# Five edits to a streaming encoder layer: silu applied in the query stage, work reordered in the first and third chunk, another bank for the latents' transposes, a later norm

## The chip, the cores and the metric

The kernel runs on one core of one Trainium2 chip. The core has a matrix engine (TensorE, PE in the profile; PEld is its weight load), a vector engine (VectorE, DVE), an activation engine (ScalarE, ACT), a general engine (GpSimd, POOL) and a sync engine (SyncE, SP) which issues most of the DMA transfers. Each has its own queue of instructions; the engines meet at semaphores. TensorE writes into PSUM, which here is divided into eight banks: four named `mm`, two named `tp` and two named `g`. The metric is the device time of one execution in microseconds (us); lower is better.

## The reference

One layer of a streaming encoder, for 1024 new frames of one stream (positions from 0) and 64 frames of a running stream with 512 cached frames. The model width is 1024; the two streams lie side by side as 1088 tokens.

```
mod = silu(c) @ w_ada + b_ada              # six vectors per stream: shift, scale, gate, twice
h = rms_norm(x, g_norm1) * (1 + scale1) + shift1
proj = h @ w_in                            # c_q 384, c_kv 256, k_rope 64, gq 256, gk 256, gv 512, g_lr 16, g_r 512
latent = rms_norm(c_kv);  q = rms_norm(c_q) @ w_uq;  k, v = latent @ w_ukv     # norms per head, rotary part
a_out = chunk-causal softmax attention(q, k, v)                # 4 heads, the cached frames ahead of the new ones
b_out = rms_norm(gated linear recurrence(gq, gk, gv, gate(g_lr))) * silu(g_r)
x = x + gate1 * (concat(a_out, b_out) @ w_out)
h2 = rms_norm(x, g_norm2) * (1 + scale2) + shift2
x = x + gate2 * (square(relu(h2 @ w_up)) @ w_down)
```

It returns x for both streams, the new latents and rotary keys, and the final states of the recurrence. Everything is float32.

## The kernel before

Almost every matmul is made three times: an operand is split into a rounded high part and the rest (`split`, lines 101 to 103: a copy on ACT, a subtraction on DVE), and `mm3` (lines 92 to 96) multiplies high by high, high by low and low by high into one PSUM bank. In the last stages `w_up` and `w_down` are multiplied by a scheme with seven products of half-size blocks.

**What sets the order.** The stages are written as Python generators that yield `(PE time, wait, condition)`; `interleave` (line 47) runs them by a clock of its own, in nanoseconds, and so fixes the order in which instructions are written down. A condition is a set of names that must be in `done`. Behind this, a scheduler lays out each engine's queue: an instruction written earlier has precedence, but one whose operands and buffers it takes to be ready may go ahead. So the load of line 619, which is written behind the whole first stage, is issued at 33.83 us. An instruction inside `pin` (`keep_in_program_order`) keeps its place among the pinned ones of its engine.

**First stage** (to about 90 us). The tokens come in three chunks of 384, 384 and 320 columns (`CHUNKS`). `start` loads the first chunk of x in two halves of four blocks of 128 rows each (`load_x`, line 301), the half-matrices of `w_ada` for the scale, and the first weights of groups A0 and A1 (`load_first`). `scale_rows` and `scale_end` (lines 466 and 472) make the scale in two halves: matmuls, a copy on ACT (line 474), a transpose on PE (line 478) and three small DVE operations that leave the gain G. Then `gained_x` (line 379) multiplies x by G into `hh` (ACT, line 383) and `hl` (DVE, line 384); `split_first` (line 324) splits weights (lines 328 and 329); `squares` (line 332) makes the squares of x on ACT and `adds` (line 338) sums them over the eight blocks on DVE (line 342); `scales` (line 345) turns the sums into the factor of the norm. `shifts` (line 491) makes the shift vector: `mod_vec` (line 158) loads rows of `w_ada` (line 165), three ahead, and multiplies them one after another (line 177); it also issues the load of the third chunk of x. `qk` (line 528) makes the first matmuls of all, for gq and gk.

**Recurrence, keys and queries** (about 90 to 350 us). `gate_cols` (line 676) makes the 512 columns of g_r and stores them in DRAM as `r_d`, unchanged. `latents` (line 686) normalises c_kv of one tile of 128 tokens after another, transposes it (line 710) into a PSUM bank, copies it out with a gain (line 713) and stores it. `past_keys` and `new_keys` make keys and values, with transposes into `tp` banks (lines 1001 and 1008). `query_main` (line 1321) makes c_q, 384 columns at a time. Small buffers of this stage lie in the pool `qp` (line 1355).

**Attention and output** (about 350 to 690 us). `attend` (line 1068) makes scores, their exponentials on ACT (line 1090), transposes of these (line 1116) and the product with the values. `out_early` (line 1273) and `main` (line 1411) load the mixed heads and `r_d`, apply silu to the latter and multiply (`gate`, line 1269), split the result and multiply it by `w_out`, in four parts of 272 tokens in the order `WORDER = (0, 2, 1, 3)`. While a part is made, squares of the new x are summed into `acc` (line 1465). `norm2` (line 1469) waits until a part is done and a time more, sums `acc` over the partitions on PE (line 1479) and spreads the factor of the norm (line 1490).

**Feed-forward** (about 690 us to the end). The seven products of `w_up` and of `w_down`; the diff does not touch them.

Of the kernel before, what the change touches and what calls it, by code (L numbers as in the profile page):

```python
# [19 lines left out]
P = 128  # L20
# [52 lines left out]
def layer(ctx: ExitStack, tc: tile.TileContext, I, O):  # L73
# [9 lines left out]
    def mm_bank():  # L83
        return psA.tile([P, 512], F32, name="mm")

    def tp_bank():
        return psT.tile([P, 512], F32, name="tp")
# [147 lines left out]
    def has(*keys):  # L235
        return lambda: all(k in done or k in groups for k in keys)
# [59 lines left out]
    with ExitStack() as sctx:  # L296
# [4 lines left out]
        def load_x(c, ks=(0, 4)):  # L301
            c0, cn = CHUNKS[c]
            for k in ks:
                SP.dma_start(hf[:, k:k + 4, c0:c0 + cn],
                             I["x_T"][k * P:(k + 4) * P, c0:c0 + cn].rearrange("(k p) n -> p k n", p=P))
# [18 lines left out]
        def split_first(hf, j, us=None):  # L324
            for u in us or (2 * hf, 2 * hf + 1):
                wh, wl = groups[GROUPS[j][0]]
                hi, lo, raw = wh[:, 2 * u:2 * u + 2], wl[:, 2 * u:2 * u + 2], first.pop((j, u))
                pin(ACT.copy(hi, raw))  # L328
                pin(DVE.tensor_tensor(out=lo, in0=raw, in1=f32(hi), op=ALU.subtract))
                done.add(f"split {j} {u}")  # L330

        def squares(c, sq, ks):

            c0, cn = CHUNKS[c]
            for k in ks:
                pin(ACT.activation(sq[:, k:k + 4, :cn], hf[:, k:k + 4, c0:c0 + cn], AF.Square))
# [42 lines left out]
        def gained_x(k, c, pin=lambda mm: mm):  # L379

            for s, a, b in spans(c):
                x, g = hf[:, k, a:b], G12[:, 0, k, s:s + 1]
                pin(ACT.activation(h["h"][:, k, a:b], x, AF.Copy, scale=g))
                mm = DVE.scalar_tensor_tensor(out=h["l"][:, k, a:b], in0=x, scalar=g, in1=f32(h["h"][:, k, a:b]),
                                              op0=ALU.mult, op1=ALU.subtract)
                if c == 0:
                    pin(mm)

        def start():
            load_mod(0)  # L390
            load_x(0, (0,))
            load_first(0)
            load_mod(1)
            load_x(0, (4,))
            load_first(1)
            yield 0, 100, None
            load_x(1)
            acc = g_bank()
            for j in range(2):
                groups[GROUPS[j][0]] = [wp.tile([P, 8, 256], F32R, name=n) for n in ("wh", "wl")]  # L400
            for k in range(0, KT, 2):
                scale_rows(0, acc, (k, k + 1))
                turn(4 if k < 6 else 1)
            scale_end(0, acc)
            turn(10)
            for n in "hl":
                h[n] = hpool.tile([P, KT, TOK + 2], F32R, name="h" + n)
            sq = xp.tile([P, KT, 384], F32, name="sq", bufs=2)
            for k in range(4):
                gained_x(k, 0, pin)  # L410
                if k % 2 == 0:
                    split_first(0, 0, (k // 2,))
            split_first(0, 1)
            squares(0, sq, (0,))
            adds(0, sq, ((0, 2), (0, 1)), pin)
            done.add("h 0 0")
            yield 0, 0, has("mod 1 1")
            squares(0, sq, (4,))
            for k in range(4, KT):
                gained_x(k, 0, pin)  # L420
                if k % 2 == 0:
                    split_first(1, 0, (k // 2,))
            done.add("h 0")
            adds(0, sq, ((4, 2), (4, 1)), pin)
            split_first(1, 1)
            yield 0, 0, None
            sums = scales(0, sq)
            yield next(sums)
            yield next(sums)
            for k in range(KT):  # L430
                gained_x(k, 1, pin)
            done.add("h 1")
            yield from sums
            sqs = {}
            for c in (1, 2):
                sqs[c] = xp.tile([P, KT, 384], F32, name="sq", bufs=2)
            squares(1, sqs[1], (0, 4))
            yield 0, 1500, None
            sums = scales(1, sqs[1])
            yield next(sums)  # L440
            yield 0, 0, has("x 2")
            squares(2, sqs[2], (0, 4))
            yield from sums
            yield from scales(2, sqs[2])
            normed(2)
            yield 0, 0, has("shift")
            for k in range(KT):
                shifted(2, k)
                done.add(f"h 2 {k}")
                yield 0, 300, None  # L450
# [40 lines left out]
        def shifts():  # L491


            yield 0, 1000, has("split 1 3")
            vec = mod_vec(0, rawp, "raw", dp, mm_bank, 3, after=1000)
            yield next(vec)
            load_x(2)
            SP.dma_start(wg[0:16], I["w_gate_up"])
            SP.dma_start(wg[96:97], I["b_gate_up"])
            SP.dma_start(indi, I["gla_ind"])  # L500
            done.add("x 2")
            yield from vec
            sh = modT[:, 0]
            split(h["h"][:, :, TOK:], h["l"][:, :, TOK:], sh, DVE)
            done.add("shift")
            for c in range(2):
                yield 2000, 0, has(f"qk {c}", "h 2 7" if c == 0 else "B1")
                for k in range(KT):
                    normed(c, (k,))
                    shifted(c, k)  # L510
                    yield 0, 300, None
# [96 lines left out]
    with gctx:  # L608
# [77 lines left out]
        def latents():  # L686
            yield 2000, 0, has("D1")
            for i in (8, 0, 1, 2, 3, 4, 5, 6, 7):
                off, n = TILES[i]
                s = i == 8  # L690
                ps = yield from rows("D1", off, n, 320)
                cn_ = dp.tile([P, 256], F32, name="cn")
                s2 = dp.tile([P, 2], F32, name="s2")
                ACT.activation(cn_[:n], ps[:, 0:256], AF.Square, accum_out=s2[:n, 0:1])
                rstd(s2[:n, 1:2], s2[:n, 0:1], n, 1, 1.0 / 256)
                DVE.tensor_scalar(out=cn_[:n], in0=ps[:, 0:256], scalar1=s2[:n, 1:2], scalar2=None, op0=ALU.mult)
                ki = 12 if s else i
                ACT.copy(kraw[:n, ki], ps[:, 256:320])
                lat = dp.tile([P, 256], F32, name="lat", bufs=1)
                DVE.tensor_tensor(out=lat[:n], in0=cn_[:n], in1=gkv_bc[:n], op=ALU.mult)  # L700
                ol, ok = (O["lat_s"], O["kr_s"]) if s else (O["lat_p"], O["kr_p"])
                oo = 0 if s else off
                ACT.dma_start(ol[oo:oo + n], lat[:n])
                SP.dma_start(ok[oo:oo + n], kraw[:n, ki])
                tails.append((i, off, n, cn_))
                while len(tails) > (0 if i == 7 else 1):
                    j, o2, n2, c2 = tails.pop(0)
                    tp = tp_bank()
                    for b in range(2):
                        PE.transpose(tp[:, b * P:b * P + n2], c2[:n2, b * P:(b + 1) * P], ident[:n2, :n2])  # L710
                    cl = dp.tile([P, 2, P], F32, name="cl", bufs=1)
                    for b in range(2):
                        ACT.activation(cl[:, b, :n2], tp[:, b * P:b * P + n2], AF.Copy, scale=gkvT[:, b:b + 1])
                    SP.dma_start(lat_d[:, :, o2:o2 + n2], cl[:, :, :n2])
                    done.add(f"lat {j}")
                    yield 220, 1500, None
            done.add("end D1")
# [549 lines left out]
        return [mixh[0].tile([P, 8, HW], F32R, name=f"m{x}0") for x in "hl"]  # L1267

    def gate(t, r):
        ACT.activation(r, r, AF.Silu)  # L1270
        DVE.tensor_tensor(out=t, in0=t, in1=r, op=ALU.mult)

    def out_early():
# [41 lines left out]
    def query_latents():  # L1315

        for g in range(3):
            yield from load_group(f"Q{g}", w_in_cols(P * g, P * g + P), 8, P, step=4, pool=qp,
                                  after=None if g < 2 else has("end Q0"))

    def query_main():
# [30 lines left out]
            done.add(f"end Q{g}")  # L1352
        sums(*pend.pop())

    with tc.tile_pool(reuse_waits="tile", name="qp", bufs=2) as qp:
        interleave([weights, past_keys(), lats, query_main(), query_latents()], rest=(weights,))
    hctx.close()
    tabq = attn_pool("tabq", 1).tile([P, 8, 2, 64], F32, name="tabq")
    rotary_table(tabq, 0)
# [37 lines left out]
    with ExitStack() as octx:  # L1397
# [71 lines left out]
        def norm2():  # L1469
            for c in WORDER:  # L1470
                h, hs, parts = place(c)
                end = c == WORDER[-1]
                yield 0, 0, has("up" if end else f"x2 {c}")
                yield 0, 2500 if end else 4500, None
                acc = sums.pop(c)
                blocks = ((0, P), (P, P), (2 * P, HW - 2 * P))
                pm = tp_bank()
# [515 lines left out]
```

## Time and profile before

| | |
|---|---|
| three runs | 1344.54, 1346.70 and 1346.73 us; median 1346.7 |
| the profiled execution's own time | 1345.33 us |
| its span, first to last instruction | 1343.2 us |
| mean granted TensorE clock | 0.999 |
| DMA moved | 183.63 MB, mean 137 GB/s |

The profiled execution takes 2.1 us beyond its span. In rows of the timeline the first two numbers are the start and the duration in us, then come the engine (with a q for its sequencer or a DMA issue), the line, the operation, its output and inputs, their shapes, and in brackets the idle time ahead of it and what ended it. In rows of stretches `A:B` come the length, then for PE, PEld, DVE, ACT and POOL the busy time with the count of instructions, then the granted clock, the DMA share and GB/s. In rows of instruction groups the three numbers after the count are the shortest, median and longest duration in ns, then the first and last start.

### The profile page before, as it was taken

How to read it: one execution, taken by the hardware profiler on the slowest of the kernel's cores; microseconds unless marked ns; L12 is line 12 of the kernel's file. 1: busy time of each engine (PE TensorE's matmuls, PEld its weight loads, DVE VectorE, ACT ScalarE, POOL GpSimd, SP SyncE). 2: the span in 40 equal slices, each digit the busy share in tenths (PEclk: the TensorE clock that was granted, in tenths of full speed). 3: DMA queues.
4: the chain of work that ended last, by engine and by line, in shares of the span. 5: the costliest groups of instructions: out<-in, count | busy, mean ns of one | idle time of the engine just before them, and what ended most of it. 6: DMA issues, size and time to landing. Idle time of an engine off the chain costs nothing.

```text
span 1343.2 us, 25901 instructions
## 1 busy us (share of the span) xinstructions
PE 1320.6 (98%) x10052; PEld 1255.2 (93%) x10052; DVE 891.1 (66%) x1920; ACT 653.5 (49%) x1626; POOL 75.9 (6%) x136
## 2 busy tenths in 40 slices
PE   9999999999999999999999999999999999999999
PEld 8799999888767888999999999999999999999998
DVE  4898787456576756677799566575646865864553
ACT  5375554444256656753575444445443343334332
POOL 0000010131112200000000000000000000000000
PEclk9999999999999999999999999999999999999999
DMA  9420122334445320682427444444259755443441
GB/s 343 143 75 1 48 76 88 105 93 124 144 141 179 94 87 17 172 238 77 138 65 244 132 156 139 136 157 131 112 184 364 246 166 187 157 127 91 134 126 34
DMA packets 153525, 183.63 MB, mean 137 GB/s; under 512 B 14478, under 2 KB 104890, under 8 KB 153402
## 3 DMA queue, kind: packets, MB, share of 16 engines
q1 hardware_dynamic: 146122, 176.46, 41.1%
q10 hardware_dynamic: 7280, 5.52, 1.3%
q8 instruction: 79, 1.29, 0.4%
q14 instruction: 44, 0.36, 0.1%
HBM read 130.71 MB, written 51.23 MB: 135 GB/s over the span
## 4 chain that ended last, share of the span: by engine, by line
PE 83%; DVE 7%; DMA 3%; ACT 3%; issue 1%; POOL 1%; SPq 0%; ACTq 0%; DVEq 0%; POOLq 0%
PE mm L94 15%; PE mm L96 14%; PE mm L95 14%; PE g L94 6%; PE g L96 6%; PE g L95 5%; PE mm L1079 3%; PE tp L94 3%; PE tp L96 3%; PE tp L95 3%; PE g L1106 2%; PE g L881 2%; PE tp L1116 1%; PE mm L177 1%; PE mm L130 1%
## 5 line engine op out<-in xcount | busy, mean ns | idle before, releaser
L102 ACT CAST opers<-quad 128x512 fp32r<-128x512 f32 x112 | 69.4, 620 | 184.2 <-PE mm L96 147.9
L103 DVE TENSOR_TENSOR opers<-quad,opers 128x512 fp32r<-128x512 f32 x112 | 77.2, 689 | 114.3 <-ACT opers L102 114.3
L96 PE MATMUL mm<-opers 128*128 128x272 f32 x448 | 128.7, 288 | 0.0
L94 PE MATMUL mm<-opers 128*128 128x272 f32 x448 | 128.4, 287 | 0.3 <-DVE e L1922 0.3
L95 PE MATMUL mm<-opers 128*128 128x272 f32 x448 | 128.2, 286 | 0.0
L94 PE MATMUL mm<-ah,wh 128*128 128x272 f32 x424 | 121.9, 288 | 0.0
L96 PE MATMUL mm<-ah,wl 128*128 128x272 f32 x424 | 121.8, 288 | 0.0
L95 PE MATMUL mm<-al,wh 128*128 128x272 f32 x424 | 121.7, 287 | 0.0
L94 PE MATMUL mm<-hh,wh 128*128 128x384 f32 (+2 forms) x264 | 91.0, 345 | 0.7 <-ACT wh L328 0.7
L95 PE MATMUL mm<-hl,wh 128*128 128x384 f32 (+2 forms) x264 | 87.2, 330 | 0.0
L96 PE MATMUL mm<-hh,wl 128*128 128x384 f32 (+2 forms) x264 | 86.7, 330 | 0.0
L94 PEld LDWEIGHTS mm<-opers 128*128 128x128 f32 x448 | 84.5, 189 | 0.5 <-issue 0.5
L96 PEld LDWEIGHTS mm<-opers 128*128 128x128 f32 x448 | 84.2, 188 | 0.0
L95 PEld LDWEIGHTS mm<-opers 128*128 128x128 f32 x448 | 84.0, 187 | 0.0
L94 PEld LDWEIGHTS mm<-ah,wh 128*128 128x128 f32 x424 | 79.9, 188 | 0.0
L95 PEld LDWEIGHTS mm<-al,wh 128*128 128x128 f32 x424 | 79.8, 188 | 0.0
L96 PEld LDWEIGHTS mm<-ah,wl 128*128 128x128 f32 x424 | 79.6, 188 | 0.1
L103 DVE TENSOR_TENSOR opers<-ru,opers 128x544 fp32r<-128x544 f32 x108 | 77.5, 718 | 2.3 <-ACT opers L102 2.0
L102 ACT CAST opers<-ru 128x544 fp32r<-128x544 f32 x108 | 69.4, 643 | 13.2 <-PE mm L96 10.9
L102 ACT CAST wh<-ru 128x512 fp32r<-128x512 f32 x67 | 41.1, 619 | 71.1 <-PE g L95 21.2
L103 DVE TENSOR_TENSOR wl<-ru,wh 128x512 fp32r<-128x512 f32 x67 | 45.6, 688 | 35.4 <-ACT wh L102 35.2
L94 PE MATMUL mm<-wh,hh 128*128 128x264 f32 (+3 forms) x216 | 65.7, 304 | 0.0
(410 smaller groups left out, 4245.1 us busy)
## 6 DMA issues: line engine op xcount, KB each, us to landing
ru<-u_d SPq DMA_DIRECT2D x108, 272.0 KB, 2.8
raw<-in_w_ada SPq DMA_DIRECT2D x40, 512.0 KB, 4.3
ru<-in_w_up SPq DMA_DIRECT2D x32, 512.0 KB, 4.1
quad<-in_w_down SPq DMA_DIRECT2D x16, 1024.0 KB, 6.6
u_d<-st SPq DMA_DIRECT2D x60, 272.0 KB, 2.1
u_d<-sc SPq DMA_DIRECT2D x45, 272.0 KB, 2.2
raw<-in_w_in SPq DMA_DIRECT2D x22, 256.0 KB, 3.5
x<-in_xo_T SPq DMA_DIRECT2D x8, 544.0 KB, 5.3
```

The costliest lines, as they stand in the source:

```text
L94: pin(PE.matmul(out, lhsT=ah, rhs=bh, start=first, stop=False, skip_group_check=more))
L95: pin(PE.matmul(out, lhsT=ah, rhs=bl, start=False, stop=False, skip_group_check=more))
L96: pin(PE.matmul(out, lhsT=al, rhs=bh, start=False, stop=last, skip_group_check=more))
L102: ACT.copy(hi, src)
L103: eng.tensor_tensor(out=lo, in0=src, in1=f32(hi), op=ALU.subtract)
L130: pin(PE.matmul(busy[:, 0:P], lhsT=ones, rhs=ones, start=True, stop=True))
L177: mm = PE.matmul(acc[32 * j:32 * j + 32, 0:256], lhsT=scT[:, k, :], rhs=was[k][:, 256 * j:256 * (j + 1)], start=(k == 0), stop=(k == KT - ...
L881: PE.matmul(sc[:n, a, p], lhsT=d[:, w * p + n * a:w * p + n * a + n], rhs=qv[:, :, p, a], start=True, stop=True)
L1079: PE.matmul(sp[:n, :w], lhsT=x[:, hd, :n], rhs=y[:, hd, :w], start=(j == 0), stop=(j == 4))
L1106: PE.matmul(op[:n, 0:P], lhsT=pt[:kw, k, :n], rhs=kvs[kt // 4].v[:kw, kt % 4, hd], start=(kt == 0), stop=(kt == nkt - 1))
L1116: PE.transpose(tp[:kw, k, :n], pr[k0 // 4][:n, P * k:P * k + kw], ident[:n, :n])
```

## The change

Five edits.

1. In `start`, the squares of the second half of the first chunk are written ahead of the wait for the second half of the scale, and each cast of weights ahead of the product with the gain.
2. In `shifts`, only the first half of the third chunk is loaded at once; the second half and three small loads are issued after the loop over the rows of `w_ada` has given five steps, which is behind the loads of rows 3 to 5.
3. In `latents`, the transposes go into a bank of `mm` instead of `tp`.
4. `gate` no longer applies silu. A new generator, `gates`, in the stage of the queries, loads `r_d` in four pieces of 272 tokens (each 128 x 4 x 272), applies silu and stores each piece back to where it was.
5. `norm2` waits 8000 instead of 4500 behind the first part, 0.

```diff
@@ start
             done.add("h 0 0")
+            squares(0, sq, (4,))
             yield 0, 0, has("mod 1 1")
-            squares(0, sq, (4,))
             for k in range(4, KT):
-                gained_x(k, 0, pin)
                 if k % 2 == 0:
                     split_first(1, 0, (k // 2,))
+                gained_x(k, 0, pin)
@@ shifts
             yield next(vec)
-            load_x(2)
-            SP.dma_start(wg[0:16], I["w_gate_up"])
-            SP.dma_start(wg[96:97], I["b_gate_up"])
-            SP.dma_start(indi, I["gla_ind"])
-            done.add("x 2")
-            yield from vec
+            load_x(2, (0,))
+            for n, step in enumerate(vec):
+                yield step
+                if n == 4:
+                    load_x(2, (4,))
+                    SP.dma_start(wg[0:16], I["w_gate_up"])
+                    SP.dma_start(wg[96:97], I["b_gate_up"])
+                    SP.dma_start(indi, I["gla_ind"])
+                    done.add("x 2")
@@ latents
-                    tp = tp_bank()
+                    tp = mm_bank()
@@ gate
     def gate(t, r):
-        ACT.activation(r, r, AF.Silu)
         DVE.tensor_tensor(out=t, in0=t, in1=r, op=ALU.mult)
@@ stage of the queries
+    def gates():
+
+        yield 0, 0, has("k 8", "end C1")
+        for c in range(4):
+            r = qp.tile([P, 4, HT // 2], F32, name="r", bufs=2)
+            ts = slice(c * HT // 2, (c + 1) * HT // 2)
+            SP.dma_start(r, r_d[:, :, ts])
+            yield 0, 3500, None
+            ACT.activation(r, r, AF.Silu)
+            SP.dma_start(r_d[:, :, ts], r)
+            yield 0, 1000, None
+
     with tc.tile_pool(reuse_waits="tile", name="qp", bufs=2) as qp:
-        interleave([weights, past_keys(), lats, query_main(), query_latents()], rest=(weights,))
+        interleave([weights, past_keys(), lats, query_main(), query_latents(), gates()], rest=(weights,))
@@ norm2
-                yield 0, 2500 if end else 4500, None
+                yield 0, {WORDER[0]: 8000, WORDER[-1]: 2500}.get(c, 4500), None
```

## The prediction

> **What bounds the kernel now.** I read the page's first lines, then the waits of TensorE alone, then the timeline at each wait that an edit touches. The page says that there is little to win.
>
> ```profile
> span 1343.2 us, 25901 instructions
> PE 1320.6 (98%) x10052; PEld 1255.2 (93%) x10052; DVE 891.1 (66%) x1920; ACT 653.5 (49%) x1626; POOL 75.9 (6%) x136
> ```
>
> TensorE (PE) is busy for 1320.6 of 1343.2 us. All its idle time is 22.6 us, and nothing in the diff takes a matmul away, so the change can only win back pieces of those 22.6 us and what the clock lost around them. The waits of PE, summed over the execution (columns: line, what released it, us in total, times, longest):
>
> ```profile
> PE tp L1116 <- ACT prob L1090: 2.3, 3, 1.2
> PE tp L1479 <- DVE acc L1465: 1.6, 1, 1.6
> PE tp L1008 <- ACT cl L713: 1.3, 1, 1.3
> PE mm L177 <- DMA raw<-in_w_ada: 1.3, 2, 0.8
> ...
> PE mm L94 <- ACT wh L328: 0.7, 1, 0.7
> PE tp L710 <- ACT mog L830: 0.6, 1, 0.6
> ```
>
> Each edit answers one of these rows: L94 (squares and weights ahead), L177 (half a load behind rows), L1008 and L710 (the bank of the latents' transposes), L1116 (silu moved), L1479 (8000 for 4500). I cost them in the order of time.
>
> **First chunk, 22 to 27 us.** The squares of the chunk's second half, one ACT instruction of 128x1536, go ahead of the copy at line 474 that carries the second half of the scale; both are pinned in program order. Two weight casts go ahead of the products with the gain.
>
> ```profile
> L304 SPq DMA_DIRECT2D hf<-in_x_T x1: 367/367/367, 12.5 to 12.5; - x1
> DMA to landing us min/median/max: 10.4/10.4/10.4
> 23.17 0.27 ACT L474 COPY lat<-g 128x128 f32<-128x128 f32 x1 [4.90 <-PE g L469]
> 23.33 1.49 ACT L336 ACTIVATE sq<-hf 128x1536 f32<-128x1536 f32 x1
> 24.13 0.27 PE L478 MATMUL tp<-ident,lat 128*128 128x128 f32 x1
> 25.05 0.62 ACT L383 ACTIVATE hh<-hf,G 128x384 fp32r<-128x384 f32 x1 [0.23 <-DVE G L488]
> 25.57 0.60 ACT L328 CAST wh<-raw 128x512 fp32r<-128x512 f32 x1
> 26.23 0.44 PE L94 MATMUL mm<-hh,wh 128*128 128x384 f32 x1 [0.66 <-ACT wh L328]
> ```
>
> ACT idles 4.90 us before the copy, which looks like free room for 1.49 us of squares. It is not: the squares read the half of x that was issued at 12.5 and lands 10.4 later, at 22.9. So they run from 22.9 to 24.4 and the copy behind them ends near 24.6, where it ended at 23.44. The transpose at 24.13 waits until about 24.65, so PE idles 0.5 us there; the gain G, for which the product at 25.05 waits, is ready half a microsecond later, near 25.5; the cast (0.60) now fits between, so the first product with the gain is done near 26.1 and PE starts its next matmul near 26.2, where it starts now. The wait of 0.66 becomes one of 0.5 and a rest of 0.1. I take 0, with bounds from -0.66 (the transpose is covered) to +0.5 (both waits are paid).
>
> **Third chunk behind the rows, 28 to 90 us.** The second half of chunk 2 and three small loads are issued behind the loads of the rows 3 to 5 of the shift.
>
> ```profile
> 28.99 0.44 SPq L304 DMA_DIRECT2D hf<-in_x_T  x1
> 32.25 0.34 SPq L165 DMA_DIRECT2D raw<-in_w_ada  x1
> 37.90 8.37 SPq L165 DMA_DIRECT2D raw<-in_w_ada  x5
> 39.87 5.63 DVE L342 TENSOR_TENSOR sq<-sq 128x1536 f32<-128x1536 f32 x6
> 42.59 0.64 PE L177 MATMUL mm<-raw,scT 128*32 128x256 f32 x8 [0.53 <-DMA raw<-in_w_ada]
> 45.25 0.64 PE L177 MATMUL mm<-raw,scT 128*32 128x256 f32 x8 [0.76 <-DMA raw<-in_w_ada]
> 60.00:90.00 30.00, 29.70 (x209) 29.49 (x208) 29.64 (x72) 19.95 (x49) 0.75 (x2) 1.00 0.17 42
> ```
>
> Row 2, issued at 32.25, no longer stands behind the half chunk, so the rows 3 to 5, whose buffers come free only as the rows 0 to 2 are used, can start a little sooner. At best both waits go: -1.3 (0.53 + 0.76). What is late next is the half chunk itself: it goes from 28.99 to behind the last of the three loads that begin at 37.90, some 10 us later, and its squares and half of the six additions of L342 (5.63 / 2, about 2.8 us of DVE) go with it. Behind them wait the chunk's scale, its normalised tokens and the matmuls on them; rows 6 and 7 are queued behind the half chunk too. The stretch from 60 to 90 has no room for that: PE is busy 29.70 and DVE 29.64 of 30 us. If all of the additions end up on the path it is +2.8. I take -0.5: the additions find idle DVE time before 60 more often than not, but only part of the two waits can go.
>
> **Bank of the latents' transposes, 256 to 330 us.** The `tp` pool has two banks, shared with the keys' transposes; the `mm` pool has four. The wait at L1008 for the copies `cl` (1.3) is a wait for a `tp` bank, and so is that of L710 for `mog` (0.6). Both can go: -1.9 at best.
>
> ```profile
> L713 ACT ACTIVATE cl<-tp,vT x18: 313/366/385, 262.8 to 315.5; 128x128 f32<-128x128 f32 x16, 128x64 f32<-128x64 f32 x2
> ```
>
> The price is that an `mm` bank is held for two of these copies, 0.73 us, nine times; a matmul group of rows or columns that found no bank would wait that long once: +0.7. I take -1.3: the long wait goes, the short one is followed at once by data that is not ready.
>
> **Silu moved, 250 to 380 and 550 to 600 us.**
>
> ```profile
> L1270 ACT ACTIVATE mr<-mr x3: 1112/1115/1115, 577.6 to 597.0; 128x1088 f32<-128x1088 f32 x3
> 550.22 1.28 ACT L1270 ACT_TABLE_LOAD   x1 [0.45 <-DMA raw<-r_d]
> 551.52 0.66 ACT L1270 ACTIVATE raw<-raw 128x544 f32<-128x544 f32 x1
> 552.19 1.28 ACT L1090 ACT_TABLE_LOAD   x1
> 554.41 0.66 PE L1116 MATMUL tp<-ident,prob 128*128 128x128 f32 x4 [0.87 <-ACT prob L1090]
> 585.29 1.11 ACT L1270 ACTIVATE mr<-mr 128x1088 f32<-128x1088 f32 x1 [3.08 <-DMA mr<-r_d]
> mr<-r_d SPq DMA_DIRECT2D x2, 544.0 KB, 4.7
> 580.00:590.00 10.00, 9.26 (x74) 9.04 (x72) 6.06 (x9) 4.36 (x7) 0.00 (x0) 1.00 0.73 218
> 260.00:340.00 80.00, 75.56 (x466) 69.39 (x465) 46.49 (x122) 35.02 (x132) 18.48 (x36) 1.00 0.36 104
> ```
>
> Removed at 550: a table load, a silu and the load of the exponential's table, 3.22 us between two softmaxes (1.28 + 0.66 + 1.28). PE waited 0.87 for it, and that goes: -0.87, at worst 0. The later silus (1.11 each) stand before no wait of PE; the other waits of L1116 (2.3 - 0.87) lie ahead of the first silu and stay. Added: four silus of the same 128x1088, 4.46 us, one table load, and one load back before the first softmax, 7.0 us of ACT in all; and eight transfers of about 544 KB, 4.7 us each. Between 260 and 340 ACT is busy 35.02 of 80 us and the DMA engines 0.36, so there is room, and the loads have no reader but the silu. But ACT stands idle in front of a silu whose load is late, as at 585.29, and PE waits for ACT often in the keys' stage. I charge +0.9: half of one silu with its table load (1.11 + 1.28, halved is 1.2) less what the other waits cover. The low end is 0; the high end is a rival below.
>
> **Norm, 589 us.** The sum over chunk 0 enters PE's queue 3500 units later.
>
> ```profile
> 590.89 0.71 PE L1479 MATMUL tp<-ones,acc 128*128 128x1 f32 x6 [1.64 <-DVE acc L1465]
> 592.00:593.00 1.00, 1.00 (x7) 1.00 (x6) 0.46 (x2) 1.00 (x1) 0.00 (x0) 0.55 1.04 323
> 593.00:594.00 1.00, 1.00 (x7) 1.00 (x6) 1.00 (x4) 0.52 (x2) 0.69 (x1) 0.50 0.76 113
> 594.00:595.00 1.00, 1.00 (x6) 1.00 (x6) 0.48 (x1) 0.00 (x0) 1.00 (x1) 0.50 0.86 202
> 595.00:596.00 1.00, 1.00 (x8) 1.00 (x7) 0.86 (x4) 0.00 (x0) 0.59 (x2) 0.75 1.05 371
> ```
>
> Two losses. PE waits 1.64, and 3.5 us of other matmuls now cover that. Then the granted clock (the column before the DMA share) falls to 0.55, 0.50, 0.50 and 0.75 for four microseconds, right behind the wait: 0.45 + 0.50 + 0.50 + 0.25 = 1.70 us of matmul time lost. I read the drop as made by the wait together with the 0.71 us of one-column matmuls, and let both go: -3.34, with bounds 0 and -3.34. [...]
>
> **The sum.** 0 - 0.5 - 1.3 - 0.87 + 0.9 - 3.34 = -5.1 us. Against the profiled execution's own 1345.33 this is 1340.2. That execution lies 1.4 under the median of the three runs (1346.7), from which the sum gives 1341.6. I predict the middle, 1340.9.
>
> **Rivals.**
> - *The waits go, the clock does not* (0.14). The drop has its own cause, or another short wait makes one elsewhere: without the 1.70 the sum is 1341.9 from the profiled time and 1343.3 from the median, about 1342.6. For it: one drop beside one wait is thin evidence. Against it: it begins a microsecond behind the longest wait on the list.
> - *Given back* (0.24). PE's next wait takes the place of the one removed: the transposes at L1008 and L710 find their operands late, and the half chunk's additions (+2.8) go through the stretch from 60 to 90. For it: 0.7 at L94 already only moves, and DVE has 0.36 us free there. Then -5.1 + 1.3 + 0.5 + 2.8 is -0.5, so 1344.8 to 1346.2.
> - *Slower: silu at the head of ACT's queue waits for its load* (0.14). The place is the keys' stage, 255 to 350 us. Each of the four silus waits as the one at 585.29 does, 3.08 us, with the copies and casts for keys and latents behind it, for which PE waits: up to 12.3 us. Without the 0.9 the gains are 6.0, so it decides from 1.5 us per load. At three quarters of the price, 9.2, the time is 1345.3 - 6.0 + 9.2, about 1348.5. Against it: the DMA engines were 0.73 full from 580 to 590 and are 0.36 full here.
> - *The change does not do what it says* (inside "given back"): without pinning, a silu may be laid out anywhere from 255 to 370 us; if between softmaxes, it keeps its table loads, and the -0.87 is lost.
>
> **How the numbers follow.** The forecast has 0.48; its own range is 1338.0 to 1343.0. A measurement of this kernel can tell about 0.2%, 2.7 us, from no change. Faster by that: the forecast, the first rival, 0.62. Same: "given back", 0.24. Slower: 0.14. With every gain at its bound and no cost, -0.66 - 1.3 - 1.9 - 0.87 - 3.34 is -8.1, or 1337.2; from there, with room for a new order of the queues, to a middling case of the slower rival: 1336.5 to 1347.5.
>
> **What would show it.** Right: no wait at L1479 and a granted clock of 1.00 from 590 to 600; no L1270 table loads near 550; no wait at L1008 for `cl`; the silus on ACT before 350. The first chunk is right if the copy at L474 ends near 24.6 and PE waits there. Wrong: a silu with several microseconds of waiting for `r_d` in front of it and PE waiting behind; DVE late beyond 90 us; a new drop of the clock.

## The result, and the profile after

The changed kernel takes 1342.76 us (median of 13 runs, 1342.39 to 1344.55); the kernel before, timed beside it, 1345.31 (13 runs, 1344.02 to 1346.97). The ratio is 0.9979, with a 95% interval of 0.9971 to 0.9986: faster by 1.9 to 3.9 us. The forecast was 1340.9. The sign was right, and about half of the forecast 5.1 us came. The profiled executions say the same: 1343.18 us against 1345.33, -2.15.

The head of the page after the change, and the waits of TensorE by what released them (us in total, times, longest):

```profile
span 1341.1 us, 25907 instructions
PE 1320.1 (98%) x10052; PEld 1253.8 (93%) x10052; DVE 891.4 (66%) x1920; ACT 651.7 (49%) x1624; POOL 75.2 (6%) x136
```

```profile
PE tp L1119 <- ACT prob L1093: 2.7, 4, 1.2
...
PE tp L1156 <- DVE kl L1006: 1.1, 3, 0.8
PE mm L713 <- DVE cn L699: 1.0, 1, 1.0
...
PE g L1109 <- DVE pt L1122: 0.8, 1, 0.8
PE tp L1504 <- DVE dg L1500: 0.7, 1, 0.7
PE mm L177 <- DMA raw<-in_w_ada: 0.7, 1, 0.7
...
PE tp L478 <- ACT lat L474: 0.3, 1, 0.3
```

All six rows that the edits aimed at have changed. Gone are the wait for `acc` (1.6), those for `cl` (1.3) and `mog` (0.6), and that for `wh` (0.7). New are waits for `pt`, `dg` and `lat`; those for `kl` have grown from 0.2 to 1.1, that for `cn` from 0.8 to 1.0, and those for `prob` from 2.3 to 2.7.

**Where the time moved.** To place gains and losses I matched each TensorE instruction of one trace with the same one in the other (same source text, operands and count) and took the difference of their starts; the table holds the median over the instructions of the 10 us that begin at the time above it. A number that falls along a row is time won there.

```
start minus start in the trace before, us, for instructions from
             20    240    300    360    380    540    570    650   1300 us
changed    +0.71  -0.73  -2.10  -1.78  -0.60  -1.13  -0.21  -2.67  -2.14
again      -0.14  -0.91  -2.22  -2.22  -1.02  -1.40  -0.82  -4.22  -3.76
start_only +0.33  -0.37  -0.29  +0.01  +0.03  -0.15  -0.45  -1.68  -1.21
rows_only  +1.02  -0.41  -0.33  -0.03  -0.04  -0.29  -0.54  -0.35  +0.19
bank_only  +0.52  -0.62  -2.72  -2.44  -2.44  -2.55  -2.39  -2.14  -1.85
silu_only  +0.97  -0.04  +1.52  +1.59  +2.79  +3.28  +3.59  +0.89  +1.47
norm_only  +0.42  -0.69  -0.66  -0.40  -0.38  +0.04  +0.29  -1.14  -1.21
no_silu    +0.48  -0.59  -2.75  -2.46  -2.46  -2.74  -2.97  -4.85  -4.66
norm_two   +0.62  +0.09  +0.09  +0.13  +0.14  +0.67  +0.44  -2.59  -1.89
wait_two   -0.09  -0.38  -2.53  -2.55  -2.55  -2.27  -2.08  -4.93  -4.24
table_back +0.55  -1.49  -2.84  -2.58  -2.58  -2.51  -1.46  -4.73  -4.09
gate_pool  +0.17  -1.16  -2.54  -2.27  -2.27  -1.83  -0.49  -3.88  -3.29
```

The row `again` is a second profile of the changed kernel (changed_again, below). The row `rows_only` is the yardstick: that kernel runs the program of before (below), and still drifts, by 1.4 in the first stretch, where the loads of the start land, and by half a microsecond behind it. Behind 240 us a step of half a microsecond is noise; one of about a microsecond that recurs in several rows is not. The stretch from 570 to 650 is an exception: start_only, which has no edit there, moves by -1.2 in it; its granted clock is 1.00 in every slice from 585 to 610, where the clock of the kernel before took 1.70 us. In the changed kernel there are four: -1.4 between 240 and 300, **+1.2 between 360 and 380, +0.9 between 540 and 570**, and -2.5 between 570 and 650. The second profile has -1.3, +1.2, +0.6 and -3.4. The two that lose are both places of the silu edit.

**The silus in the query stage.** ScalarE, and the stretch from 260 to 340 us (busy time of PE, PEld, DVE, ACT and POOL, granted clock, DMA share):

```profile
268.30 1.28 ACT L1365 ACT_TABLE_LOAD   x1
269.59 1.12 ACT L1365 ACTIVATE r<-r 128x1088 f32<-128x1088 f32 x1
...
284.96 1.11 ACT L1365 ACTIVATE r<-r 128x1088 f32<-128x1088 f32 x1 [0.34 <-DVE rt L973]
```

```profile
260.00:340.00 80.00, 76.89 (x470) 70.58 (x469) 47.88 (x123) 40.22 (x138) 18.57 (x36) 1.00 0.53 160
```

None of the four waits for its load. The DMA share rises from 0.36 to 0.53, ScalarE's busy time by 5.2 us. The waits for `kl` come with the silus: they are 1.1 here, and 0.2 in bank_only and no_silu (below), which have the other bank and no silus in this stage.

**The first softmax.** ScalarE's timeline before it, and the wait of TensorE there:

```profile
371.34 1.28 ACT L1093 ACT_TABLE_LOAD   x1
372.64 0.77 ACT L1093 ACTIVATE prob<-mm,sta,ssq 64x512 f32<-64x512 f32 x1
```

```profile
373.56 0.46 PE L1119 MATMUL tp<-ident,prob 64*128 64x64 f32 x4 [1.10 <-ACT prob L1093]
```

ScalarE loads a table ahead of the first silu, at 268.30, and no other until the softmax's first exponential, which stands some 80 us behind the last silu; the load there takes 1.28 us, while TensorE waits 1.10. In the kernel before, the softmax's only load is the one at 552.19, behind a silu. The prediction counted the load before the first softmax among ScalarE's 7.0 us, but put no wait of TensorE to it.

**The gates at 550.** VectorE, ScalarE and TensorE after the change:

```profile
554.15 0.73 DVE L1273 TENSOR_TENSOR raw<-raw 128x544 f32<-128x544 f32 x1 [1.42 <-DMA raw<-r_d]
...
554.93 0.69 DVE L1122 COPY pt<-tp 128x512 f32<-128x512 f32 x1
```

```profile
554.92 0.65 ACT L102 CAST mh<-raw 128x544 fp32r<-128x544 f32 x1 [1.94 <-DVE raw L1273]
```

```profile
555.67 0.94 PE L1109 MATMUL g<-v,pt 128*128 128x128 f32 x6 [0.77 <-DVE pt L1122]
```

The tables and silus are gone from ScalarE, as forecast. But without them the load of `r` for the second gate is itself what comes last. The multiply waits 1.42 for it at the head of VectorE's queue, with the softmax's small steps and the copy `pt` behind it, and the cast of the product waits 1.94 at the head of ScalarE's, with the next `prob` (555.73) behind it. In the kernel before, this multiply stood at 559.93 and VectorE waited as long for it, 1.68; but TensorE did not wait there. What is new is that the multiply comes between the steps of a softmax. These waits don't carry the whole loss: from 545 to 565 TensorE is busy for 18.91 us here and was for 19.13 before, 0.2 of the +0.9. The rest lies in TensorE's busy time, in another order of the matmuls, and its cause stays open.

**The norm.** The two matmul steps of the norm over chunk 0, and one of the slices in which the clock had been at 0.50 (granted clock ahead of the DMA share):

```profile
591.91 0.63 PE L1493 MATMUL tp<-ones,acc 128*128 128x1 f32 x6
596.45 1.00 PE L1504 MATMUL tp<-dg,ones 128*128 128x128 f32 x6 [0.69 <-DVE dg L1500]
```

```profile
594.00:595.00 1.00, 1.00 (x10) 1.00 (x10) 0.44 (x2) 0.50 (x2) 0.00 (x0) 1.00 1.03 326
```

No wait at the sum, and a granted clock of 1.00, here and in the slices around. The next step of the same norm waits 0.69 for `dg`, which is made from that sum; in the second profile of this kernel (changed_again) it doesn't wait:

```profile
594.98 0.93 PE L1504 MATMUL tp<-dg,ones 128*128 128x128 f32 x6
```

### The profile page after: what moved, and what is told of

It is laid out like the page before. It is cut to its first block, busy times and chain, and to the rows that moved or that the text cites. A ratio compares the mean times of both kernels' runs of the same rounds, so it can differ in the third digit from the quotient of the medians.

```text
span 1341.1 us, 25907 instructions
## 1 busy us (share of the span) xinstructions
PE 1320.1 (98%) x10052; PEld 1253.8 (93%) x10052; DVE 891.4 (66%) x1920; ACT 651.7 (49%) x1624; POOL 75.2 (6%) x136
## 4 chain that ended last, share of the span: by engine, by line
PE 83%; DVE 7%; DMA 3%; ACT 3%; issue 2%; POOL 1%; ACTq 0%; SPq 0%; DVEq 0%; POOLq 0%
PE mm L94 14%; PE mm L96 14%; PE mm L95 14%; PE g L94 6%; PE g L96 6%; PE g L95 5%; PE tp L94 3%; PE tp L96 3%; PE mm L1082 3%; PE tp L95 3%; PE g L1109 2%; PE g L884 2%; PE tp L1119 1%; PE mm L177 1%; DVE wl L106 1%
```

## The experiments

Ratios are against the kernel before, timed in the same comparison; the last column is the interval in us.

| kernel | time, us | before, us | ratio (95%) | difference, us |
|---|---|---|---|---|
| changed (second comparison) | 1342.22 | 1345.89 | 0.9977 (0.9967 to 0.9988) | -4.4 to -1.6 |
| start_only | 1345.41 | 1345.80 | 1.0000 (0.9991 to 1.0009) | -1.2 to +1.2 |
| rows_only | 1345.32 | 1345.80 | 0.9994 (0.9985 to 1.0003) | -2.0 to +0.4 |
| bank_only | 1343.74 | 1345.84 | 0.9983 (0.9974 to 0.9992) | -3.5 to -1.1 |
| silu_only | 1346.01 | 1345.84 | 1.0002 (0.9993 to 1.0010) | -0.9 to +1.3 |
| norm_only | 1344.52 | 1345.84 | 0.9993 (0.9984 to 1.0001) | -2.2 to +0.1 |
| no_silu | 1342.38 | 1345.84 | 0.9971 (0.9960 to 0.9983) | -5.4 to -2.3 |
| norm_two | 1343.33 | 1345.89 | 0.9981 (0.9973 to 0.9990) | -3.6 to -1.3 |
| wait_two | 1339.53 | 1345.89 | 0.9955 (0.9943 to 0.9968) | -7.7 to -4.3 |
| table_back | 1341.23 | 1345.89 | 0.9966 (0.9953 to 0.9978) | -6.3 to -3.0 |
| gate_pool | 1343.95 | 1345.80 | 0.9983 (0.9975 to 0.9992) | -3.4 to -1.1 |
| wait_long | 1347.97 | 1345.80 | 1.0017 (1.0008 to 1.0026) | +1.1 to +3.5 |

### The first chunk alone

The kernel before with the first hunk of the diff.

> The kernel before with the first chunk's edit alone. Theory as predicted: 0, with bounds from -0.66 to +0.5; in the profile the squares at line 336 end after the copy's old end at 23.4, the copy at line 474 ends near 24.6, TensorE waits some 0.3 to 0.5 us at line 478 and less than 0.2 for wh. Rival (the weight casts ahead win more than that, as the shift of -0.9 from 50 us on in the changed kernel may be read): -0.9 or more, with both waits short.

ScalarE and TensorE of start_only:

```profile
23.42 1.49 ACT L336 ACTIVATE sq<-hf 128x1536 f32<-128x1536 f32 x1 [4.83 <-DMA hf<-in_x_T]
24.82 0.25 ACT L474 COPY lat<-g 128x128 f32<-128x128 f32 x1
```

```profile
25.12 0.33 PE L478 MATMUL tp<-ident,lat 128*128 128x128 f32 x1 [0.49 <-ACT lat L474]
```

The squares wait for their half of x, the copy behind them ends at 25.07, and the old wait for `wh` (0.66) is replaced by one of 0.49 for `lat`: the mechanism is as predicted, half a microsecond later than reckoned, since the half of x comes at 23.4 in this execution and not at 22.9. The time is 0.0 +- 1.2. A gain of 0.9 or more isn't excluded by that interval, but nothing in these waits would carry it.

### The rows alone

The kernel before with the second hunk.

> The kernel before with the rows' edit alone. Read off the instruction streams, this kernel issues the same instructions in the same order on every engine and queue as the kernel before: the chunk's second half still stands right behind row 1. Theory: 0, whatever the comparison shows is what this measurement makes of no change. Rival, the prediction's term: -0.5, with bounds -1.3 and +2.8; the waits of L177 for the rows would be gone, and the half chunk would be issued behind row 5, near 40 us.

-2.0 to +0.4: no change, as it must be for the same program: on every engine and queue its trace has the instructions of the kernel before in the same order. The queue SP of the changed kernel shows the same, and can be set beside the rows of before in the prediction:

```profile
29.12 0.44 SPq L304 DMA_DIRECT2D hf<-in_x_T  x1
32.92 0.34 SPq L165 DMA_DIRECT2D raw<-in_w_ada  x1
...
38.51 1.29 SPq L165 DMA_DIRECT2D raw<-in_w_ada  x3
```

The half chunk stands ahead of row 2 and of the rows 3 to 5, where it stood, and not behind them, as the description of the change has it. The lines were written in another place; the order in which they are issued isn't that of the text. The row of L177 in the waits (1.3 before, 0.7 after) moves by itself: in wait_long, which has no edit at the start, it is 0.7 too.

### The bank alone

`tp = mm_bank()` in place of `tp = tp_bank()` for the latents' transposes.

> The kernel before with the other bank for the latents' transposes alone. Theory as predicted: -1.3, 1344.0; the wait at L1008 for cl is gone. Rival (TensorE waits for the keys kl and the query's copies cn instead, as the changed kernel shows with 0.8 and 1.1): 0, 1345.3. Since this kernel keeps the short delay of the sum over chunk 0, its profile also shows whether the granted clock falls near 592 again: theory yes, 0.5 to 0.75 for about four microseconds; rival no drop.

-3.5 to -1.1, and by the table of shifts -2.1 between 240 and 300: it won what the prediction gave as its best bound (-1.9), not the -1.3 that it took. Both waits, for `cl` (1.3) and for `mog` (0.6), are gone from its list. The rival was that waits for `kl` and `cn` take their place: `kl` stays at 0.2, `cn` goes from 0.8 to 1.1, and 0.4 for `latl` is new. This kernel still has the early sum, and the clock falls behind its wait again. Its waits, and its windows:

```profile
588.75 0.71 PE L1479 MATMUL tp<-ones,acc 128*128 128x1 f32 x6 [1.89 <-DVE acc L1465]
```

```profile
590.00:591.00 1.00, 1.00 (x8) 1.00 (x7) 0.77 (x5) 1.00 (x2) 0.10 (x1) 0.59 0.79 226
591.00:592.00 1.00, 1.00 (x6) 1.00 (x6) 1.00 (x1) 0.27 (x1) 1.00 (x2) 0.50 0.85 103
592.00:593.00 1.00, 1.00 (x6) 1.00 (x5) 0.94 (x5) 0.00 (x0) 0.69 (x1) 0.50 0.83 256
593.00:594.00 1.00, 1.00 (x7) 1.00 (x7) 0.48 (x2) 0.43 (x1) 0.00 (x0) 0.70 1.07 384
```

0.41 + 0.50 + 0.50 + 0.30 is 1.71 us, as large as the 1.70 of before.

### The silu edit alone, and the change without it

```diff
     def gate(t, r):
-        ACT.activation(r, r, AF.Silu)
         DVE.tensor_tensor(out=t, in0=t, in1=r, op=ALU.mult)
...
-        interleave([weights, past_keys(), lats, query_main(), query_latents()], rest=(weights,))
+        interleave([weights, past_keys(), lats, query_main(), query_latents(), gates()], rest=(weights,))
```

> The kernel before with the silu edit alone. Theory: +2.0 us (+1.2 at the first softmax, +0.9 at the gate's multiply), 1347.3 against 1345.3. Rival, the prediction's own terms (-0.87 at 550, +0.9 in the query stage): 0, 1345.3. Second rival, silus that wait in ACT's queue for their loads: above 1348, with microseconds of waiting for the load in front of a silu.

> The changed kernel (1342.8 us) with its silu edit taken back: the silus stand again at line 1270's place near 550 us, and nothing is added in the query stage. Theory (the silu edit is a loss: TensorE's time against the kernel before shifts by +1.2 us near 372, where the first softmax now waits for the exponential's table, and by +0.9 near 550, where the gate's multiply on VectorE waits for its load): about 2 us faster than the changed kernel, 1340.7, that is -4.6 against the kernel before; no wait at 372 above that of the kernel before, and the shift from 540 to 580 stays level. Rival (the silu edit saves its 0.87 and the shifts come from the other edits): 1343.6, 0.9 slower than the changed kernel, with both shifts still there.

silu_only takes +0.3 (-0.9 to +1.3) where the theory had +2.0. That is the first rival's time, but not for its reason, as the shifts show. It loses 3.6 us by 570, more than the theory said (1.6 of it between 240 and 300, where the clock falls, as the last section shows; 1.2 at the first softmax, but only 0.3 at the gates), and **wins 2.7 back between 570 and 650**, though the sum over chunk 0 stands where it stood. Its TensorE at the norm:

```profile
592.68 0.63 PE L1490 MATMUL tp<-ones,acc 128*128 128x1 f32 x6
596.99 1.00 PE L1501 MATMUL tp<-dg,ones 128*128 128x128 f32 x6 [0.46 <-DVE dg L1497]
```

There is no wait for `acc` left. In the kernel before, the silu at 585.29 waited 3.08 us for its load with the squares for `acc` behind it in ScalarE's queue, and VectorE's addition to `acc` waited for these:

```profile
586.30 0.41 ACT L1464 ACTIVATE sq<-x 128x272 f32<-128x272 f32 x1
586.75 0.44 DVE L1465 TENSOR_TENSOR acc<-acc,sq 128x272 f32<-128x272 f32 x1 [2.44 <-ACT sq L1464]
```

The silu edit takes that silu away, and with it the wait that the norm's edit was made for: **two edits had the same 3.3 us to win, and it is won once.** The prediction's sentence that the later silus "stand before no wait of PE" was wrong, and the row that shows it was quoted beside it.

no_silu takes 1342.38 us, where the theory had 1340.7 and the rival 1343.6. Its shifts follow the theory: level between 360 and 380 and between 540 and 570, and at the end 2.5 us ahead of the changed kernel's first profile, 0.9 ahead of its second. Its time doesn't decide: -5.4 to -2.3 overlaps with the changed kernel's -3.9 to -1.9. Its executions differ in the clock, which comes next.

### The norm alone, and its second wait

```diff
-                yield 0, 2500 if end else 4500, None
+                yield 0, {WORDER[0]: 8000, WORDER[-1]: 2500}.get(c, 4500), None
```

That is norm_only. norm_two has besides, ahead of the matmul into `bc`:

```diff
-                yield 0, 3000, None
+                yield 0, 5000 if c == WORDER[0] else 3000, None
```

> The kernel before with the later sum over chunk 0 alone. Theory as predicted: the wait of 1.64 and the clock's 1.70 both go, less a wait of about 0.7 us for the scaled identity (dg) at the next step, -2.6, 1342.7. Rival (the clock's drop is in only some executions, or has its own cause): -0.9, 1344.4, with a granted clock below 1.00 between 590 and 600 in this profile or none in the profile of a kernel that keeps the 4500.

> The kernel before with the later sum over chunk 0, and the step behind it (the scaled identity's matmul into bc) 5000 units later instead of 3000. With the sum alone later (norm_only), TensorE waited 1.7 us for dg in the profile, and 5 of 11 executions had a mean granted clock below 1.000 and were some 2 us longer than the 6 at 1.000. Theory (the wait and the clock belong together; the edit only moved the wait to the next step): without that wait nothing is left near 596, every execution has a clock of 1.000, and the prediction's -3.3 is reached: 1342.5 where the kernel before has 1345.8. Rival (the wait moves on again, to the scaled products or to dg of the next chunk, or the drops in some executions lie elsewhere): -1.3 as norm_only, 1344.5, with executions below 1.000.

norm_only wins 0.9 (-2.2 to +0.1), not 2.6: the rival's time, and as the rival had it the clock falls in only some executions. The wait moved from the sum to the next step with nearly its whole length. norm_only, then no_silu, which has the same edit:

```profile
597.98 1.00 PE L1490 MATMUL tp<-dg,ones 128*128 128x128 f32 x6 [1.72 <-DVE dg L1486]
```

```profile
594.28 1.00 PE L1493 MATMUL tp<-dg,ones 128*128 128x128 f32 x6 [1.28 <-DVE dg L1489]
```

In both profiles the clock stays at 1.00. But not in all of their other executions: 5 of 11 of norm_only have a mean granted clock below 1.000, at 1346.4 us on average where the six at 1.000 have 1343.8, and 4 of 7 of no_silu, 1343.1 against 1340.7. With the second step later as well, norm_two has no wait there, all its 11 executions are at 1.000, and it wins 2.6 (-3.6 to -1.3): by the shifts -3.0 between 570 and 650, where the prediction had -3.34.

### No silu edit, and no second wait

no_silu with norm_two's second line, and without the rows' hunk.

> The kernel without the silu edit, with the first chunk's, the bank's and the sum's edits and with bc 5000 units later for chunk 0. Without the later bc (no_silu) it had a wait of 1.3 for dg in the profile, 4 of 7 executions below a clock of 1.000, a median of 1342.4 and 1340.7 for the executions at 1.000. Theory: dg's wait goes with the clock's drops, 1339.5, -6.3 against 1345.8, every execution at 1.000. Rival (drops in some executions come from other waits): 1341 to 1342 with the same spread of clocks.

1339.53 us, as expected, with all five executions at a clock of 1.000. This is faster than both kernels: 4.3 to 7.7 us under the kernel before, where the changed kernel of the same comparison is 1.6 to 4.4 under it. What is left at the norm in its profile:

```profile
595.71 1.00 PE L1490 MATMUL tp<-dg,ones 128*128 128x128 f32 x6 [0.31 <-DVE dg L1486]
```

### The changed kernel again, and its two losses mended one by one

> The changed kernel once more, beside the three others. Theory: its waits near 590 are short (0.7 for dg), so that no execution has a clock below 1.000, and the executions lie within about 1 us of each other: 1342.8 against 1345.8. Rival: as in the kernels with one edit, a third or more of the executions are below 1.000, and the median against the kernel before is -1.5 or less.

1342.22 us; 7 of 8 executions at 1.000, and none of the 13 of the first comparison below. The clock came nearly as expected, the spread didn't: the executions lie between 1341.06 and 1344.88, 3.8 us apart and not 1, and the seven at 1.000 alone span 2.3 us. What spreads them stays open.

table_back calls the exponential's table back where nobody waits:

```diff
             SP.dma_start(r_d[:, :, ts], r)
+            if c == 3:
+                back = qp.tile([P, 1], F32, name="back", bufs=1)
+                ACT.activation(back, r[:, 0, 0:1], AF.Exp, scale=0.0)
```

> The changed kernel with one exponential of a single column behind the fourth silu in the query stage, so that the exponential's table is loaded there and not in front of the first softmax. Theory: the wait of 1.1 us for prob near 372 goes, and with it 1.1 us of the time against the changed kernel, 1341.7 where that has 1342.8. Rival (the wait is that of the exponential itself or of the scores, as in the kernel before, and a table load near 290 delays the keys instead): no change or +1, 1342.8 to 1343.8.

ScalarE of table_back, behind the silus and at the first softmax:

```profile
288.96 1.28 ACT L1369 ACT_TABLE_LOAD   x1
290.26 0.20 ACT L1369 ACTIVATE back<-r 128x1 f32<-128x1 f32 x1
```

```profile
370.44 0.77 ACT L1093 ACTIVATE prob<-mm,sta,ssq 64x512 f32<-64x512 f32 x1
```

No table load and no wait at the softmax, and the shift is level there. 1341.23 us, 1.0 under the changed kernel of the same comparison. The two intervals overlap, so that the size rests on the trace (+1.2 against 0.0 between 360 and 380). The load takes the same 1.28 us at 289, but costs TensorE nothing that the shifts show: -1.35 between 240 and 300, where the changed kernel has -1.37.

gate_pool is table_back with the second gate's multiply on GpSimd (the call; `gate` now takes the engine as a third argument):

```diff
-        gate(t2, r2)
+        gate(t2, r2, POOL)
```

> The changed kernel with the exponential's table called back (table_back) and the second of the two gate multiplies near 550 us on GpSimd instead of VectorE; apart from that multiply, VectorE's order changes by one reciprocal. Theory (the loss near 550 is VectorE's queue standing behind the multiply that waits for its load of r): the wait of L1109 for VectorE near 554 goes, about -1 us against table_back, 1340.2, with the shift from 540 to 580 level. Rival (the attention there waits for its own scores, or the casts that need the product now stand behind a slower multiply): 1341.2 or more, with another wait near 555.

The theory fell and the rival came, a wait near 555 behind a slower multiply: 1343.95 us, and +1.3 between 540 and 570 where table_back has +1.1. GpSimd, ScalarE, TensorE:

```profile
553.22 1.33 POOL L1273 TENSOR_TENSOR raw<-raw 128x544 f32<-128x544 f32 x1 [24.55 <-DMA raw<-mix_d]
554.58 0.65 ACT L102 CAST mh<-raw 128x544 fp32r<-128x544 f32 x1 [2.63 <-POOL raw L1273]
556.05 0.66 PE L1119 MATMUL tp<-ident,prob 128*128 128x128 f32 x4 [1.95 <-ACT prob L1093]
```

VectorE's queue is free, but ScalarE's cast of the product waits 2.63 us instead of 1.94, with the exponentials behind it. Part of that is GpSimd itself, which takes 1.33 us for the multiply where VectorE took 0.73. So the run shows that this move doesn't help, and not what an equally fast multiply off VectorE's queue would do. That the late data are the cause is argued from the waits; an earlier load of `r`, which would settle it, wasn't tried.

### A longer wait

norm_only with the second step 500 units behind the first instead of 3000.

> The kernel before with the later sum over chunk 0, as norm_only, but with the step behind it 500 units later instead of 3000, so that TensorE comes to dg's matmul earlier and waits longer there: about 3 us by the some 1.7 us of matmuls that no longer stand in front, where norm_only waited 1.7. Theory (whether the granted clock falls goes by the length of the wait and by its place against something that runs free of the program): all or nearly all executions are below 1.000, where norm_only had 5 of 11, and the median is 3 us or more above norm_only's, 1347.5 or more. Rival (the clock falls because of the one-column matmuls behind the sum's wait, not of a wait): the share below 1.000 stays at a half or less, and only the longer wait is paid, 1346.

1347.97 us, 3.5 above norm_only, and all 11 executions below 1.000. The wait, and the windows behind it:

```profile
597.27 1.73 PE L1490 MATMUL tp<-dg,ones 128*128 128x128 f32 x6 [3.31 <-DVE dg L1486]
```

```profile
596.00:597.00 1.00, 0.00 (x0) 0.00 (x0) 0.24 (x3) 1.00 (x1) 0.90 (x2) 0.63 0.91 285
597.00:598.00 1.00, 0.73 (x3) 0.76 (x4) 0.54 (x3) 0.11 (x1) 0.35 (x1) 0.50 1.07 377
...
602.00:603.00 1.00, 1.00 (x7) 1.00 (x6) 0.97 (x3) 1.00 (x2) 0.00 (x0) 0.50 0.00 0
603.00:604.00 1.00, 1.00 (x9) 1.00 (x9) 1.00 (x2) 0.97 (x3) 0.00 (x0) 0.95 0.00 0
```

0.50 holds for the six slices from 597 to 603: 0.37 + 6 x 0.50 + 0.05 is a shortfall of 3.42 us, twice the 1.71 of bank_only. It begins while TensorE still waits (no matmul from 596 to 597, 0.73 us of them in the next slice), so about 2.9 us of it is matmul time lost. Of the theory, the length of the wait is shown; the part on its place, no run tests.

## Why the prediction was right, and where it was wrong

The sign and the largest term held; two terms of the sum, silu and rows, were wrong, and a third, the bank, was too small. In part it was luck that the time still lay in the forecast's range, near its upper edge: the bank's and the silus' errors point opposite ways. The number of the first rival, 1342.6, lies nearer to the measured 1342.76 than the forecast, but not its mechanism, since the clock held in all 13 executions.

| term | predicted | shown |
|---|---|---|
| first chunk | 0 | 0.0 +- 1.2; the waits as described |
| rows | -0.5 | 0: the queue is unchanged |
| bank | -1.3 | -2.1 by the shifts of bank_only; -3.5 to -1.1 timed |
| silu gone at 550 | -0.87 | +0.9 (second profile +0.6, silu_only +0.3) |
| silu added | +0.9 | +0.7 in the query stage, +1.2 at the first softmax |
| norm | -3.34 | -2.5 (second profile -3.4); norm_only wins 1.4 there, norm_two 3.0, and the silu edit alone 2.7 |

- **Silu** is the step that failed, by 2.8 us: +2.8 (0.9 + 0.7 + 1.2) in place of +0.03. At the norm 0.6 of that comes back, the wait for `dg` being 0.69 and not no_silu's 1.28; in the second profile, without that wait, all of the 1.28. The 0.7 is the difference of the changed kernel's step between 240 and 300 (-1.4) and bank_only's (-2.1); so the charge in the query stage was right, and the slower rival (silus that wait for loads there) didn't come. Wrong were "that goes: -0.87, at worst 0", where the load of `r` took the tables' place as the last to come in the middle of a softmax (the waits account for 0.2 of the +0.9, the rest is open), and the load back before the first softmax: it was counted as busy time of ScalarE, for which there was room, and not as a wait of TensorE. table_back shows that this wait, +1.2, goes when the load stands elsewhere. The rival "does not do what it says" had the loss of the 0.87, but not the way.
- **Norm**: the mechanism held. The wait at the sum went, and the clock with it. The size came in the second profile, -3.4, and not in the first, where the next step of the same norm waits 0.69 for `dg`. The term left that step out: where the silu edit is missing, it waits 1.72 (norm_only) and 1.28 (no_silu). The term was also not the norm edit's alone, since the silu edit wins most of it by itself. And its clock part was not a loss of every execution: of the 80 executions of the kernel before beside the experiments, 63 have a mean granted clock below 1.000 (last section).
- **Rows**: the step "issued behind the loads of the rows 3 to 5" is in the text of the diff and not in the queue. The bounds -1.3 and +2.8 had nothing to stand on.
- **Bank**: right in kind, mis-sized by 0.8 on the careful side. The prediction took it that the short wait, for `mog`, would be followed at once by one for data that are not ready; in bank_only both waits went, and less came in their place: 0.3 more for `cn` and 0.4 for `latl`.
- **First chunk**: as worked out.

## What to carry to other kernels

A table switch and the way back were two loads of 1.28 us here, one in front of the silus and one in front of the exponentials (268.30 and 371.34 in the changed kernel); cost each where it falls: the second cost TensorE 1.1 at the first softmax and nothing that the shifts show where table_back has it, at 289 us. Where two edits relieve one chain of queues, cost them together, and after moving the first step of a chain move its later steps as well, or the wait only moves on. And read a reordering off the queue, since where a line is written may decide nothing.

## What the runs showed of the hardware

The granted clock fell behind waits of 1.6 to 1.9 us in a part of the executions, and behind one of 3.3 us in all 11. Listed are the longest wait of TensorE in each kernel's profile, and its executions with a mean granted clock below 1.000:

| kernel | longest wait, us | below 1.000 |
|---|---|---|
| before | 1.6 | 63 of 80 |
| bank_only, start_only, rows_only | 1.9, 1.8, 1.9 | 10, 9 and 6 of 11 |
| norm_only, silu_only, gate_pool | 1.7, 1.9, 1.9 | 5, 3 and 4 of 11 |
| no_silu | 1.3 | 4 of 7 |
| changed (both comparisons) | 1.2 | 1 of 21 |
| norm_two, table_back, wait_two | 1.3, 1.2, 1.5 | 0 of 21 |
| wait_long | 3.3 | 11 of 11 |

Where the longest wait is 1.2 to 1.5 us, 1 of 42 executions is below 1.000; where it is 1.6 to 1.9, 100 of 146 are, some executions of each program and not the others; at 3.3, all 11. no_silu (1.3; 4 of 7) is the exception, and single profiles stand for the lengths. That the waits are the cause, and do not only go along with the falls, is shown at the norm's second step, by which alone three kernels differ: at 500 units (wait_long) the clock falls in 11 of 11 executions, at 3000 (norm_only) in 5, at 5000 (norm_two) in none. In start_only's own profile TensorE waits 1.8 at the sum, as in bank_only's, and the clock holds behind it:

```profile
PE tp L1479 <- DVE acc L1465: 1.8, 1, 1.8
```

```profile
592.00:593.00 1.00, 1.00 (x10) 1.00 (x9) 0.71 (x5) 1.00 (x2) 0.48 (x1) 1.00 0.41 114
```

The one-column matmuls, which the prediction held for half of the cause, aren't needed for a fall. silu_only shows a fall in the keys' stage, where there are none, behind a wait for `kn`:

```profile
286.89 0.44 PE L1001 MATMUL tp<-ident,kn 128*128 128x128 f32 x2 [1.86 <-DVE kn L993]
```

```profile
287.00:288.00 1.00, 1.00 (x7) 1.00 (x8) 0.47 (x3) 0.72 (x5) 0.00 (x0) 0.72 0.88 179
288.00:289.00 1.00, 1.00 (x6) 1.00 (x5) 0.51 (x3) 1.00 (x2) 0.80 (x2) 0.50 0.97 346
289.00:290.00 1.00, 1.00 (x5) 0.79 (x3) 0.99 (x2) 1.00 (x3) 0.00 (x0) 0.50 0.08 28
290.00:292.00 2.00, 1.99 (x13) 1.79 (x13) 0.67 (x3) 0.89 (x3) 0.00 (x0) 0.78 0.61 213
```

0.28 + 0.50 + 0.50 + 2 x 0.22 is 1.72 us. Each shortfall worked out here is 1.70 to 1.72 us (the kernel before, bank_only, silu_only) or twice that (3.42, wait_long). Read as time at the 0.50 of the slices in its middle, one is 3.40 to 3.44 us at half speed, and wait_long's is 6.84: an estimate from four profiles. The waits ahead of the three single ones are 1.64, 1.89 and 1.86 us. Why one program has such a fall in some of its executions and not in others was not shown.
